# Gathered rows' vector operations pinned in source order, and the forget gates' sums moved behind the first heads' projections

## The chip, the cores and the metric

One core of one Trainium2 chip runs the whole program. The metric is the device time of one execution in microseconds (us). The engines are TensorE (PE, with its weight loads as PEld), VectorE (DVE), ScalarE (ACT), GpSimd (POOL) and SyncE (SP). Each runs its own instructions in a fixed order and waits at an instruction until what that needs is there.

## What is computed

Two transformer blocks over 512 tokens of width 1024 (D) behind 16 meta tokens. The part that matters first is the PEER layer: every token chooses 128 of 16384 experts (8 heads, 16 each); an expert is a row of the table u and a row of the table v. The first block ends with it; the second begins with a SwiGLU (ffn1) and then attention, eight heads of it with a forget gate.

```python
def peer_experts(xc, idx, gates, u, v):
    u_sel = jnp.take(u, idx, axis=0)
    act = jax.nn.gelu(jnp.einsum("chkd,cd->chk", u_sel, xc))
    v_sel = jnp.take(v, idx, axis=0)
    return jnp.einsum("chk,chkd->cd", act * gates, v_sel)
...
def fox_mixer(fq, fk, fv, f_logit, q_gain, k_gain, b_f):
...
    log_f = jax.nn.log_sigmoid((f_logit + b_f).astype(jnp.float32))
    c = jnp.cumsum(log_f, axis=1).transpose(0, 2, 1)
    out = blocked_causal_attention(to_heads(q), to_heads(k), to_heads(v), c)
    return from_heads(out)
...
        x = x + FFN_RESIDUAL_WEIGHT * swiglu(rms_norm_2(x, ffn1_norm[l]),
                                             ffn1_w_gate[l], ffn1_w_up[l], ffn1_w_down[l])
```

## The kernel before

**Three ways for four tiles.** The 512 tokens are four tiles of 128. Two of them pass through *all* experts on PE: 128 u tiles (L419, 128 experts each; the weights come as f32, ACT copies the high part into wh at L98, DVE subtracts it into wl at L103, and three products are summed) and 128 v tiles (`v_products`, the same three products), with the gates spread into a dense matrix between. The third tile (GT) has its chosen rows gathered: POOL issues an indirect DMA per choice (`fetch`, L564, 128 rows of u, then 128 of v, into four buffers named row), DVE multiplies a row of u with the token (`dot`, L570) or adds a weighted row of v to the token's sum (`add`, L580). After 16 dots ACT applies the gelu (L573). The fourth tile ("late") takes its activations out of the dense ones, which every fourth u tile spills to memory (act_d), by indirect DMAs into lact (L734); it gathers 128 rows of v (vrow, L755), and DVE adds them in `Late.add` (L744, L743 once in 16 rows). That goes on beside ffn1 and the first products of attention, until `last_tile` needs the sum.

**Stages.** Routing up to about 407 us. Then the gates stage, to about 600 us: 32 steps of eight tokens, each an oa (L622), eight ob (L625) and 16 small matmuls (L629) whose results ACT copies to stg, with u tiles between them. Then the loop: one u tile i+LAG and one v tile i per iteration, with LAG 36 (92 iterations, L668 makes the hidden values hf), and a load of gates, gt, of 1 MB every eighth iteration. SP issues the loads of weights and of gt in one queue. When the u tiles have run out, 36 iterations have v tiles alone (about 1327 to 1457 us). Behind it come the hand-over to ffn1 (a norm, whose dg at L817 PE needs), ffn1 on three tiles, the first products of attention, the late tile (about 1905 to 2045 us), and attention.

**What sets the order.** A scheduler puts each engine's instructions in order by a simulation of times, so an operation whose operand it believes to be there can go ahead of what the source has before it. `keep_in_program_order` keeps an instruction behind the one traced before it on its engine. Before, it is used for the gathers on POOL and the u tiles inside the gates stage, not for the operations that use the gathered rows. In the source the calls of `dot` and `add` are paced: one gather per step in the gates stage, then by `spent(n)`: at the loop's start 224 gathers are left, a u/v iteration counts 7 of 752 units and a v iteration 3. A row is used two gathers after its own.

**The forget gates.** In `attention`, the closures in `todo` finish the products of the last tile: `last(*todo[0])` the latents, `todo[1]` and `todo[2]` queries and keys of the gated heads, whose evacuation (`heads_norm`, L1169 to L1175: square fsq, sums, scale, four transposes) needs the scale r3m of the last tile; `todo[3]` their values. Between, DVE works off the latents' norm, the keys' rotation (krr) and a polynomial for the log of the gate (lf, up to L1251). `cp` (L1266) is the cumulative sum as four products with a triangle matrix, `c8` its copy, stored in cd (decay), and turned (L1271) into cq; both are read by the second eight heads.

Of the kernel before, what the change touches and what calls it, by code (L numbers as in the profile page):

```python
# [10 lines left out]
F32 = mybir.dt.float32  # L11
# [4 lines left out]
AF = mybir.ActivationFunctionType  # L16
ALU = mybir.AluOpType
# [3 lines left out]
P = 128  # L21
T = 512
# [410 lines left out]
def peer(c, A):  # L433
# [9 lines left out]
    with ExitStack() as es:  # L443
# [123 lines left out]

        def dot(row, s):
            jk = pe.tile([P, D], BF16, tag="jk", name="jkd", bufs=1)
            nc.vector.scalar_tensor_tensor(out=jk, in0=row, scalar=1.0, in1=xg, op0=ALU.mult, op1=ALU.mult, accum_out=gact[:, s:s + 1])  # L570
            if s % TOPK == TOPK - 1:
                hs = slice(s - TOPK + 1, s + 1)
                nc.scalar.activation(out=gact[:, hs], in_=gact[:, hs], func=AF.Gelu_apprx_tanh)  # L573

        def add(row, s):
            if s % TOPK == 0:
                hs = slice(s, s + TOPK)
                nc.vector.tensor_tensor(out=gwt[:, hs], in0=gact[:, hs], in1=G8[:, GT, s // TOPK, :], op=ALU.mult)
            hh = c.ht[GT]
            nc.vector.scalar_tensor_tensor(out=hh, in0=row, scalar=gwt[:, s:s + 1], in1=hh, op0=ALU.mult, op1=ALU.add)  # L580


        rows = []
# [135 lines left out]
class Late:  # L719
# [18 lines left out]
    def add(self):  # L738
        c, s = self.c, self.added
        if s % AHEAD == 0:  # L740
            hs = slice(s, s + AHEAD)
            a = c.lact[s // AHEAD]
            c.nc.vector.tensor_tensor(out=a, in0=a, in1=c.lg[:, hs], op=ALU.mult)  # L743
        c.nc.vector.scalar_tensor_tensor(out=self.h, in0=self.pending.pop(0), scalar=c.lact[s // AHEAD][:, s % AHEAD:s % AHEAD + 1], in1=self.h, op0=ALU.mult, op1=ALU.add)  # L744
        self.added += 1

    def steps(self, n):
# [321 lines left out]
def attention(c, A, late, late_cm):  # L1069
# [3 lines left out]
    def col(name, i=0, p=P):  # L1073
        o, n = CONST_COLS[name]
        return C[:p, o + i:o + i + 1]
# [3 lines left out]
    with ExitStack() as es:  # L1079
# [16 lines left out]
        def trp():  # L1096
            return pool.tile([P, 4, P], F32, tag="tr", name="tr", bufs=2)
# [19 lines left out]
        with tc.tile_pool(name="pre", bufs=1) as lq, tc.tile_pool(name="pret", bufs=2) as tp:  # L1117
# [30 lines left out]
            def last(w, n, evac, name="tm"):  # L1148

                ps = big(name)[:, 0:n]  # L1150
                for u in range(4):
                    wt = load_f(c, w[u], 2 * n)
                    for kk in range(2):
                        k = 2 * u + kk
                        nc.tensor.matmul(ps, xn[:, k, :], wt[:, kk * n:(kk + 1) * n], start=k == 0, stop=k == KD - 1)  # L1155
                evac(3, ps)
# [63 lines left out]
            rsqrt(c, l12, l12, (QR, KVR, ROPE))  # L1220
            for i, (o, n) in enumerate(parts):
                nc.vector.tensor_tensor(out=lat[:, :, o:o + n], in0=lat[:, :, o:o + n], in1=ls[:, i].unsqueeze(2).to_broadcast([P, 4, n]), op=ALU.mult)

            kr2 = tg.tile([P, T], F32, tag="z", name="kr2", bufs=1)
            kr = kr2[:, 0:4 * ROPE].rearrange("p (t d) -> p t d", t=4)
# [23 lines left out]
            nc.vector.tensor_tensor(out=y, in0=y, in1=z, op=ALU.mult)  # L1249
            nc.vector.tensor_scalar(out=lf, in0=lf, scalar1=0.0, scalar2=None, op0=ALU.min)  # L1250
            nc.vector.scalar_tensor_tensor(out=lf, in0=y, scalar=-2.0, in1=lf, op0=ALU.mult, op1=ALU.add)  # L1251
            last(*todo[1])
            for tt in range(4):
                ts = slice(tt * P, (tt + 1) * P)
                t4 = trp()
                nc.tensor.transpose(t4[:, 0, :], lat[:, tt, 0:P], c.ident)
                nc.tensor.transpose(t4[:QR - P, 1, :], lat[:, tt, P:QR], c.ident)
                nc.tensor.transpose(t4[:, 2, :], lat[:, tt, QR:QR + KVR], c.ident)
                for i, (p, oh, ol, g) in enumerate(((P, qnh[:, 0, ts], qnl[:, 0, ts], col("ql_g", 0)),
                                                    (QR - P, qnh[:QR - P, 1, ts], qnl[:QR - P, 1, ts], col("ql_g", 1, QR - P)),  # L1260
                                                    (P, kvh[:, ts], kvl[:, ts], col("kvl_g")))):
                    nc.scalar.activation(out=oh, in_=t4[:p, i, :], func=AF.Copy, scale=g)
                    nc.vector.scalar_tensor_tensor(out=ol, in0=t4[:p, i, :], scalar=g, in1=oh.bitcast(F32), op0=ALU.mult, op1=ALU.subtract)
            cp = big("cp")
            for j in range(4):
                nc.tensor.matmul(cp[:MH, j * P:], lf[:, j, :], tri[:, 0:T - j * P], start=(j == 0), stop=(j == 3), skip_group_check=True)  # L1266
            nc.scalar.mul(out=c8, in_=cp[:MH, :], mul=8.0)
            nc.sync.dma_start(out=cd, in_=c8)
            t4 = trp()
            for tt in range(4):  # L1270
                nc.tensor.transpose(t4[:, tt, 0:MH], c8[:, tt * P:(tt + 1) * P], c.ident[:MH, :MH])  # L1271
            nc.scalar.copy(out=cq, in_=t4[:, :, 0:MH])

            last(*todo[2])
            last(*todo[3])
            for ch in range(4):
                def evac(tt, ps):
                    z = tp.tile([P, T], F32, tag="t", name="z3", bufs=3)
# [19 lines left out]
                    nc.scalar.activation(out=dst[:, h0:h0 + 4, ts], in_=t4[:QF], func=AF.Copy, scale=col(g, 0, QF))  # L1298


            lat_cm.__exit__(None, None, None)
            wq0 = load_w(c, A["w_qb0"], n=768)
            wq1 = load_w(c, A["w_qb1"], n=768, p=QR - P)
            for tt in range(4):
# [29 lines left out]
            for tt in range(4):  # L1334
                ts = slice(tt * P, (tt + 1) * P)
                kt = tp.tile([P, MH, QF], F32, tag="qt", name="kt", bufs=2)
                ss = tp.tile([P, 2 * MH], F32, tag="ss8", name="kss", bufs=4)[:, 0:MH]
                pvs = []
                for half in range(2):
                    ps = pool.tile([P, 512], F32, tag=f"tm{tt % 2}", name="kp", bufs=1) if half else big("kp")  # L1340
                    s = slice(half * 512, half * 512 + 512)
                    mm3(nc, ps, kvh[:, ts], kvl[:, ts], wk[0][:, s], wk[1][:, s], True, True)
                    pv = ps.rearrange("p (h d) -> p h d", h=4)
                    sq = tp.tile([P, T], F32, tag="t", name="ksq", bufs=3)
                    sv = sq[:, 0:256].rearrange("p (h d) -> p h d", h=4)
                    nc.scalar.activation(out=sv, in_=pv[:, :, 0:NOPE], func=AF.Square)
                    nc.vector.tensor_reduce(out=ss[:, half * 4:half * 4 + 4], in_=sv, axis=AX.X, op=ALU.add)
                    pvs.append(pv)
                rsqrt(c, ss, ss, NOPE)
                for half, pv in enumerate(pvs):  # L1350
                    hs = slice(half * 4, half * 4 + 4)
                    nc.vector.tensor_tensor(out=kt[:, hs, 0:NOPE], in0=pv[:, :, 0:NOPE], in1=ss[:, hs].unsqueeze(2).to_broadcast([P, 4, NOPE]), op=ALU.mult)
                    nc.scalar.copy(out=vm[:, tt, hs, :], in_=pv[:, :, NOPE:])
                nc.gpsimd.tensor_copy(out=kt[:, :, NOPE:], in_=krr[:, tt:tt + 1, :].to_broadcast([P, MH, ROPE]))
                feature_major(kt, kT, "mk_g", ts)

        tp = es.enter_context(tc.tile_pool(name="att", bufs=2))
        msk = tp.tile([P, T], F32, name="msk", bufs=1)
# [240 lines left out]
```

## Time and profile before

| | |
|---|---|
| Median of 3 runs | 2746.47 us (2740.72 to 2750.86) |
| Profiled execution | 2757.47 us, its span 2755.7 us |
| Busy share of the span | PE 93%, PEld 76%, DVE 66%, ACT 33%, POOL 30% |
| Memory read and written | 534.05 MB and 31.47 MB |

A busy share is a mean over stages with different limits, so the views below cut the span into stretches. A row in the waits names the engine and line that waited, what it waited for, the sum, the number of times and the longest. In a timeline a bracket gives the idle time just ahead of an instruction and the instruction or DMA that ended it.

### The profile page before, as it was taken

How to read it: one execution, taken by the hardware profiler on the slowest of the kernel's cores; microseconds unless marked ns; L12 is line 12 of the kernel's file. 1: busy time of each engine (PE TensorE's matmuls, PEld its weight loads, DVE VectorE, ACT ScalarE, POOL GpSimd, SP SyncE). 2: the span in 40 equal slices, each digit the busy share in tenths (PEclk: the TensorE clock that was granted, in tenths of full speed). 3: DMA queues.
4: the chain of work that ended last, by engine and by line, in shares of the span. 5: the costliest groups of instructions: out<-in, count | busy, mean ns of one | idle time of the engine just before them, and what ended most of it. 6: DMA issues, size and time to landing. Idle time of an engine off the chain costs nothing. (4 is left out here: it accounts for less than half of the span.)

```text
span 2755.7 us, 33980 instructions
## 1 busy us (share of the span) xinstructions
PE 2556.0 (93%) x12098; PEld 2091.1 (76%) x12098; DVE 1812.1 (66%) x3710; ACT 915.6 (33%) x1531; POOL 823.9 (30%) x686
## 2 busy tenths in 40 slices
PE   8979988998999999999887998889988999999999
PEld 7955455787888888899666998877444877788887
DVE  7986996997878877644687987776013676443322
ACT  4232011543333333434344332333022554332221
POOL 0000244353444444100554787471000230211100
PEclk9989999999999999999998999999998799999999
DMA  4213137889999999755885888686875313222232
GB/s 169 95 61 101 62 107 276 298 284 332 345 333 339 333 324 334 268 170 178 257 282 198 292 270 279 219 293 222 299 256 169 102 36 108 90 94 94 96 103 75
DMA packets 196921, 567.77 MB, mean 206 GB/s; under 512 B 23240, under 2 KB 60488, under 8 KB 194576
## 3 DMA queue, kind: packets, MB, share of 16 engines
q1 hardware_dynamic: 132464, 355.60, 38.7%
q0 software_dynamic: 59392, 201.42, 21.1%
q10 hardware_dynamic: 4896, 8.57, 0.8%
q8 instruction: 96, 1.57, 0.2%
q14 instruction: 73, 0.60, 0.1%
HBM read 534.05 MB, written 31.47 MB: 205 GB/s over the span
## 5 line engine op out<-in xcount | busy, mean ns | idle before, releaser
L103 DVE TENSOR_TENSOR wl<-wf,wh 128x1024 fp32r<-128x1024 f32 (+2 forms) x438 | 533.7, 1219 | 276.5 <-ACT wh L98 270.5
L98 ACT CAST wh<-wf 128x1024 fp32r<-128x1024 f32 (+2 forms) x438 | 453.0, 1038 | 660.1 <-PE mm L80 207.5
L419 PE MATMUL u<-xh,wh 128*128 128x384 f32 x760 | 266.9, 351 | 33.0 <-ACT wh L98 33.0
L419 PE MATMUL u<-xh,wl 128*128 128x384 f32 x760 | 265.2, 349 | 8.5 <-DVE wl L103 8.5
L81 PE MATMUL mm<-hh,wl 128*128 128x384 f32 (+1 forms) x704 | 259.8, 369 | 8.1 <-DVE wl L103 8.0
L79 PE MATMUL mm<-hh,wh 128*128 128x384 f32 (+1 forms) x704 | 259.5, 370 | 7.2 <-ACT hh L793 3.5
L419 PE MATMUL u<-xl,wh 128*128 128x384 f32 x760 | 263.6, 347 | 0.0
L80 PE MATMUL mm<-hl,wh 128*128 128x384 f32 (+1 forms) x704 | 261.0, 371 | 0.0
L564 POOL DMA_INDIRECT row<-peer_u,gidx x128 | 180.3, 1408 | 242.4 <-DVE jkd L570 218.2
L734 POOL DMA_INDIRECT lact<-act_d,laid x128 | 157.4, 1230 | 243.9 <-DMA wf<-peer_v 205.3
L80 PE MATMUL v<-wl,hh 128*128 128x512 f32 x512 | 207.8, 406 | 15.7 <-DVE wl L103 15.3
L564 POOL DMA_INDIRECT row<-peer_v,gidx x128 | 165.1, 1290 | 179.1 <-DVE h_tok L580 151.5
L81 PE MATMUL v<-wh,hl 128*128 128x512 f32 x512 | 204.1, 400 | 0.0
L744 DVE SCALAR_TENSOR_TENSOR h_late<-vrow,lact,h_late 128x1024 f32<-128x1024 f32 x128 | 164.1, 1282 | 31.6 <-DMA vrow<-peer_v,lidx 30.9
L570 DVE SCALAR_TENSOR_TENSOR jkd<-row,xg 128x1024 bf16<-128x1024 f32 x128 | 158.2, 1236 | 38.8 <-DMA row<-peer_u,gidx 37.7
L419 PEld LDWEIGHTS u<-xh,wh 128*128 128x128 f32 x760 | 149.1, 196 | 40.5 <-ACT wh L98 36.5
L419 PE MATMUL u<-xf,w 128*128 128x384 f32 x496 | 172.7, 498 | 7.3 <-ACT spill L427 7.3
L580 DVE SCALAR_TENSOR_TENSOR h_tok<-row,gwt,h_tok 128x1024 f32<-128x1024 f32 x128 | 164.1, 1282 | 21.7 <-DMA row<-peer_v,gidx 21.2
L755 POOL DMA_INDIRECT vrow<-peer_v,lidx x128 | 153.1, 1196 | 54.9 <-issue 25.3
L419 PEld LDWEIGHTS u<-xh,wl 128*128 128x128 f32 x760 | 148.8, 196 | 14.3 <-DVE wl L103 14.0
L79 PE MATMUL v<-wh,hh 128*128 128x512 f32 x512 | 157.0, 400 | 2.5 <-ACT wh L98 2.5
L525 POOL TENSOR_TENSOR dk<-CE,posf 128x800 f32<-128x800 f32 x32 | 48.7, 1552 | 353.6 <-DVE posf L521 353.6
(437 smaller groups left out, 5311.8 us busy)
## 6 DMA issues: line engine op xcount, KB each, us to landing
wf<-peer_v SPq DMA_DIRECT2D x128, 512.0 KB, 4.6
wf<-u_t SPq DMA_DIRECT2D x95, 512.0 KB, 5.4
wf<-f_g SPq DMA_DIRECT2D x44, 512.0 KB, 3.4
wf<-f_u SPq DMA_DIRECT2D x44, 512.0 KB, 3.5
w<-u_t SPq DMA_DIRECT2D x33, 512.0 KB, 4.0
gates_d<-stg SPq DMA_DIRECT2D x16, 1024.0 KB, 7.0
gt<-gates_d SPq DMA_DIRECT2D x16, 1024.0 KB, 12.4
wf<-f_d SPq DMA_DIRECT2D x32, 512.0 KB, 3.7
```

What stands on the lines that cost most here:

```text
L79: nc.tensor.matmul(ps, lh, rh, start=start, stop=False)
L80: nc.tensor.matmul(ps, lh, rl, start=False, stop=False)
L81: nc.tensor.matmul(ps, ll, rh, start=False, stop=stop)
L98: nc.scalar.copy(out=h, in_=f)
L103: (nc.vector if lo == "v" else nc.gpsimd).tensor_tensor(out=l, in0=f, in1=h.bitcast(F32), op=ALU.subtract)
L419: mm = nc.tensor.matmul(ps3, l, r, start=k == 0 and m == 0, stop=k == KD - 1 and m == len(mms) - 1)
L564: dm = nc.gpsimd.indirect_dma_start(out=row, out_offset=None, in_=src, in_offset=bass.IndirectOffsetOnAxis(ap=gidx[:, s:s + 1], axis=0))
L570: nc.vector.scalar_tensor_tensor(out=jk, in0=row, scalar=1.0, in1=xg, op0=ALU.mult, op1=ALU.mult, accum_out=gact[:, s:s + 1])
L580: nc.vector.scalar_tensor_tensor(out=hh, in0=row, scalar=gwt[:, s:s + 1], in1=hh, op0=ALU.mult, op1=ALU.add)
L734: dm = c.nc.gpsimd.indirect_dma_start(out=c.lact[s // AHEAD][:, s % AHEAD:s % AHEAD + 1], out_offset=None, in_=acts, in_offset=bass.Indire ...
L744: c.nc.vector.scalar_tensor_tensor(out=self.h, in0=self.pending.pop(0), scalar=c.lact[s // AHEAD][:, s % AHEAD:s % AHEAD + 1], in1=self.h, ...
L755: dm = c.nc.gpsimd.indirect_dma_start(out=row, out_offset=None, in_=self.A["peer_v"], in_offset=bass.IndirectOffsetOnAxis(ap=c.lidx[:, s:s ...
```

## The change

The operations of `dot`, `add` and `Late.add` get `keep_in_program_order`, and in `attention` the calls `last(*todo[1])`, `last(*todo[2])`, the transposes of the latents and `last(*todo[3])` move ahead of the keys' rotation and the polynomial, and the cumulative sum moves behind the projections of the keys (`kp`). No instruction is added or removed. In lines of after, L570 stays, L580 is L581, L622 is L624, L668 is L670, L744 is L746, L1155 to L1203 are three higher.

```diff
         def dot(row, s):
             jk = pe.tile([P, D], BF16, tag="jk", name="jkd", bufs=1)
-            nc.vector.scalar_tensor_tensor(out=jk, in0=row, scalar=1.0, in1=xg, op0=ALU.mult, op1=ALU.mult, accum_out=gact[:, s:s + 1])
+            op = nc.vector.scalar_tensor_tensor(out=jk, in0=row, scalar=1.0, in1=xg, op0=ALU.mult, op1=ALU.mult, accum_out=gact[:, s:s + 1])
+            tc.keep_in_program_order(op)
...
             hh = c.ht[GT]
-            nc.vector.scalar_tensor_tensor(out=hh, in0=row, scalar=gwt[:, s:s + 1], in1=hh, op0=ALU.mult, op1=ALU.add)
+            op = nc.vector.scalar_tensor_tensor(out=hh, in0=row, scalar=gwt[:, s:s + 1], in1=hh, op0=ALU.mult, op1=ALU.add)
+            tc.keep_in_program_order(op)
...
-        c.nc.vector.scalar_tensor_tensor(out=self.h, in0=self.pending.pop(0), scalar=c.lact[s // AHEAD][:, s % AHEAD:s % AHEAD + 1], in1=self.h, op0=ALU.mult, op1=ALU.add)
+        op = c.nc.vector.scalar_tensor_tensor(out=self.h, in0=self.pending.pop(0), scalar=c.lact[s // AHEAD][:, s % AHEAD:s % AHEAD + 1], in1=self.h, op0=ALU.mult, op1=ALU.add)
+        c.tc.keep_in_program_order(op)
         self.added += 1
...
                 nc.vector.tensor_tensor(out=lat[:, :, o:o + n], in0=lat[:, :, o:o + n], in1=ls[:, i].unsqueeze(2).to_broadcast([P, 4, n]), op=ALU.mult)
+            last(*todo[1])
+            last(*todo[2])
+            for tt in range(4):
+                ts = slice(tt * P, (tt + 1) * P)
+                t4 = trp()
+                nc.tensor.transpose(t4[:, 0, :], lat[:, tt, 0:P], c.ident)
...
+            last(*todo[3])
 
             kr2 = tg.tile([P, T], F32, tag="z", name="kr2", bufs=1)
...
             nc.vector.scalar_tensor_tensor(out=lf, in0=y, scalar=-2.0, in1=lf, op0=ALU.mult, op1=ALU.add)
-            last(*todo[1])
-            for tt in range(4):
...
-            cp = big("cp")
...
-            last(*todo[2])
-            last(*todo[3])
...
                 feature_major(kt, kT, "mk_g", ts)
+            cp = big("cp")
+            for j in range(4):
+                nc.tensor.matmul(cp[:MH, j * P:], lf[:, j, :], tri[:, 0:T - j * P], start=(j == 0), stop=(j == 3), skip_group_check=True)
+            nc.scalar.mul(out=c8, in_=cp[:MH, :], mul=8.0)
+            nc.sync.dma_start(out=cd, in_=c8)
...
+            lat_cm.__exit__(None, None, None)
```

DVE at the start of the gates stage, before (jkd is the discarded product of a dot, gact its sum; a count at the end is of the same instruction in a row):

```order
L554 SCALAR_TENSOR_TENSOR laid<-ef,ea 128x128
L570 SCALAR_TENSOR_TENSOR jkd,gact<-row,xg 128x1024 x3
L622 TENSOR_TENSOR oa<-iota,sT 128x1024
L625 TENSOR_SCALAR ob<-iota,sT 128x128 x8
L622 TENSOR_TENSOR oa<-iota,sT 128x1024
L625 TENSOR_SCALAR ob<-iota,sT 128x128 x8
L570 SCALAR_TENSOR_TENSOR jkd,gact<-row,xg 128x1024 x10
L622 TENSOR_TENSOR oa<-iota,sT 128x1024
L625 TENSOR_SCALAR ob<-iota,sT 128x128 x8
L570 SCALAR_TENSOR_TENSOR jkd,gact<-row,xg 128x1024 x3
L578 TENSOR_TENSOR gwt<-gact,G_2044 128x16
L570 SCALAR_TENSOR_TENSOR jkd,gact<-row,xg 128x1024 x7
```

The same place after:

```order
L554 SCALAR_TENSOR_TENSOR laid<-ef,ea 128x128
L624 TENSOR_TENSOR oa<-iota,sT 128x1024
L627 TENSOR_SCALAR ob<-iota,sT 128x128 x8
L624 TENSOR_TENSOR oa<-iota,sT 128x1024
L627 TENSOR_SCALAR ob<-iota,sT 128x128 x8
L570 SCALAR_TENSOR_TENSOR jkd,gact<-row,xg 128x1024
L624 TENSOR_TENSOR oa<-iota,sT 128x1024
L627 TENSOR_SCALAR ob<-iota,sT 128x128 x8
L570 SCALAR_TENSOR_TENSOR jkd,gact<-row,xg 128x1024
```

Up to the fourth oa 23 dots stood before, and two stand now; from there each oa is followed by one. Over the stage 59 dots stood ahead of the first hf before, 35 now.

DVE in the loop at its 80th v tile, before (hf and hl are the hidden values' parts, wl a weight's low part; numbers tell the tiles apart):

```order
L668 TENSOR_TENSOR hf_9962<-act_7608,gt_9505 128x256
L103 TENSOR_TENSOR wl_9737<-wf_9734,wh_9736 128x1024
L103 TENSOR_TENSOR wl_9777<-wf_9774,wh_9776 128x1024
L103 TENSOR_TENSOR hl_9900<-hf_9897,hh_9899 128x256
L668 TENSOR_TENSOR hf_10029<-act_7675,gt_10027 128x256
L103 TENSOR_TENSOR wl_9803<-wf_9800,wh_9802 128x1024
```

The same place after:

```order
L670 TENSOR_TENSOR hf_9962<-act_7608,gt_9505 128x256
L581 SCALAR_TENSOR_TENSOR h_tok_92<-row_9724,gwt_2047,h_tok_92 128x1024
L103 TENSOR_TENSOR wl_9777<-wf_9774,wh_9776 128x1024
L581 SCALAR_TENSOR_TENSOR h_tok_92<-row_9727,gwt_2047,h_tok_92 128x1024
L103 TENSOR_TENSOR hl_9900<-hf_9897,hh_9899 128x256
L103 TENSOR_TENSOR wl_9803<-wf_9800,wh_9802 128x1024
L581 SCALAR_TENSOR_TENSOR h_tok_92<-row_9730,gwt_2047,h_tok_92 128x1024
L670 TENSOR_TENSOR hf_10029<-act_7675,gt_10027 128x256
```

Before, dots and adds came at some 2.7 per hf up to the 73rd, where 101 adds were done, and then none up to the 97th. After, they come at 2.1 per hf from the first hf to the 97th.

PE behind the late tile, before (tm products of `last`, ss the last tile's sum of squares, tl the latents, cp the cumulative sum):

```order
L1203 MATMUL ss<-ones,sqs 128x1
L1175 MATMUL tr<-ident,fsq 128x128 x4
L1256 MATMUL tr<-ident,tl 128x128
L1257 MATMUL tr<-ident,tl 64x128
L1258 MATMUL tr<-ident,tl 128x128
```

The same place after:

```order
L1206 MATMUL ss<-ones,sqs 128x1
L1158 MATMUL tm<-w_16240,xn 128x512 x2
L1158 MATMUL tm<-w_16244,xn 128x512 x2
L1158 MATMUL tm<-w_16248,xn 128x512 x2
L1158 MATMUL tm<-w_16252,xn 128x512 x2
L1178 MATMUL tr<-ident,fsq 128x128 x4
L1158 MATMUL tm<-w_16319,xn 128x512 x2
```

Sixteen products that do not need the sum of squares now stand between it and the latents' transposes, eight of them ahead of the first fsq transposes. The four cp products, which stood eight rows behind the sum of squares, come some 200 rows later.

## Rows read from the trace of the kernel before

**Rows 1.** Page, busy time by engine: us, share of the span, instructions.
```profile
PE 2556.0 (93%) x12098; PEld 2091.1 (76%) x12098; DVE 1812.1 (66%) x3710; ACT 915.6 (33%) x1531; POOL 823.9 (30%) x686
```

**Rows 2.** Stretches: length, busy PE, PEld, DVE, ACT, POOL (instructions), PEclk, DMA share, GB/s.
```profile
485.00:600.00 115.00, 115.00 (x634) 87.46 (x633) 115.00 (x291) 58.78 (x83) 51.46 (x27) 1.00 0.85 295
630.00:1146.00 516.00, 478.99 (x2345) 435.04 (x2344) 410.45 (x513) 191.72 (x335) 211.20 (x167) 0.96 0.93 331
1146.00:1327.00 181.00, 181.00 (x932) 166.72 (x931) 85.08 (x103) 73.34 (x130) 0.00 (x0) 1.00 0.58 181
1327.00:1480.00 153.00, 131.06 (x540) 102.92 (x539) 117.26 (x169) 65.27 (x102) 80.93 (x65) 0.93 0.74 241
```

**Rows 3.** Line L419 in 630 to 1146, then 1146 to 1327: min/median/max ns.
```profile
L419 PE MATMUL u<-xh,wh x518: 331/340/689, 629.5 to 1145.8; 128*128 128x384 f32 x173
...
L419 PE MATMUL u<-xh,wh x206: 334/340/343, 1145.8 to 1323.4; 128*128 128x384 f32 x103
```

**Rows 4.** Waits in 630 to 1146: us in total, times, longest.
```profile
POOL row L564 <- DVE h_tok L580: 151.0, 80, 9.9
...
PE u L419 <- ACT wh L98: 33.0, 8, 6.0
...
ACT wh L98 <- DMA wf<-u_t: 29.3, 17, 4.7
```

**Rows 5.** DMA, 600 to 1150 (last row: 1146 to 1327): queue shares; issues, us to landing.
```profile
q0 software_dynamic: 25488, 92.81, 46.6%
...
q1 hardware_dynamic: 40400, 83.14, 43.6%
...
gt<-gates_d SPq DMA_DIRECT2D x10, 1024.0 KB, 13.3
...
row<-peer_v,gidx POOLq DMA_INDIRECT x101, 7.7
...
gt<-gates_d SPq DMA_DIRECT2D x4, 1024.0 KB, 7.3
```

**Rows 6.** PE's timeline, 455 to 486: start, us, [idle <-releaser]; a wait of ACT.
```profile
456.67 7.12 PE L419 MATMUL u<-xf,w 128*128 128x384 f32 x16 [4.31 <-ACT spill L427]
...
464.07 2.75 PE L419 MATMUL u<-xf,w 128*128 128x384 f32 x8
...
477.01 3.78 PE L629 MATMUL g<-ob,oa 128*128 128x128 f32 x16 [6.05 <-DVE ob L625]
...
483.40 1.95 PE L629 MATMUL g<-ob,oa 128*128 128x128 f32 x16
...
ACT gact L573 <- DVE jkd L570: 18.3, 3, 14.7
```

**Rows 7.** Waits in 1327 to 1480; then a DVE group: busy, mean ns, idle.
```profile
DVE h_tok L580 <- DMA row<-peer_v,gidx: 17.1, 8, 7.1
...
PE v L80 <- DVE wl L103: 15.3, 9, 4.2
...
L580 DVE SCALAR_TENSOR_TENSOR h_tok<-row,gwt,h_tok 128x1024 f32<-128x1024 f32 x27 | 34.7, 1286 | 17.2 <-DMA row<-peer_v,gidx 17.1
```

**Rows 8.** Timelines of PE and DVE at the hand-over to ffn1.
```profile
1499.54 1.62 PE L818 MATMUL bc<-dg,ones 128*128 128x128 f32 x6 [11.27 <-DVE dg L817]
...
1492.18 1.28 DVE L744 SCALAR_TENSOR_TENSOR h_late<-vrow,lact,h_late 128x1024 f32<-128x1024 f32 x1 [5.66 <-DMA vrow<-peer_v,lidx]
```

**Rows 9.** Waits of PE in ffn1, 1510 to 1790.
```profile
PE dn L81 <- DVE wl L103: 13.8, 6, 4.8
PE mm L81 <- DVE wl L103: 8.0, 2, 5.8
```

**Rows 10.** PE's timeline before attention's last tile.
```profile
1862.19 1.12 PE L1175 MATMUL tr<-ident,fsq 128*128 128x128 f32 x4 [8.10 <-DVE fsq L1172]
```

**Rows 11.** PE's timeline behind the late tile.
```profile
2067.51 1.09 PE L1175 MATMUL tr<-ident,fsq 128*128 128x128 f32 x4 [11.77 <-DVE krr L1066]
...
2071.32 3.95 PE L1266 MATMUL cp<-tl,lf 128*8 128x512 f32 x6 [1.04 <-DVE lf L1251]
```

More of the change, by code (lines that the diff above doesn't have):

```diff
@@ L1222, in attention @@
                 nc.vector.tensor_tensor(out=lat[:, :, o:o + n], in0=lat[:, :, o:o + n], in1=ls[:, i].unsqueeze(2).to_broadcast([P, 4, n]), op=ALU.mult)
+            last(*todo[1])
[4 more added lines that the diff above has]
+                nc.tensor.transpose(t4[:, 0, :], lat[:, tt, 0:P], c.ident)
+                nc.tensor.transpose(t4[:QR - P, 1, :], lat[:, tt, P:QR], c.ident)
+                nc.tensor.transpose(t4[:, 2, :], lat[:, tt, QR:QR + KVR], c.ident)
+                for i, (p, oh, ol, g) in enumerate(((P, qnh[:, 0, ts], qnl[:, 0, ts], col("ql_g", 0)),
+                                                    (QR - P, qnh[:QR - P, 1, ts], qnl[:QR - P, 1, ts], col("ql_g", 1, QR - P)),
+                                                    (P, kvh[:, ts], kvl[:, ts], col("kvl_g")))):
+                    nc.scalar.activation(out=oh, in_=t4[:p, i, :], func=AF.Copy, scale=g)
+                    nc.vector.scalar_tensor_tensor(out=ol, in0=t4[:p, i, :], scalar=g, in1=oh.bitcast(F32), op0=ALU.mult, op1=ALU.subtract)
+            last(*todo[3])
             kr2 = tg.tile([P, T], F32, tag="z", name="kr2", bufs=1)
@@ L1251, in attention @@
             nc.vector.scalar_tensor_tensor(out=lf, in0=y, scalar=-2.0, in1=lf, op0=ALU.mult, op1=ALU.add)
-            last(*todo[1])
-            for tt in range(4):
[L1254 to L1263, printed above, removed]
-            cp = big("cp")
[L1265 to L1272, printed above, removed]
-            last(*todo[2])
-            last(*todo[3])
             for ch in range(4):
@@ L1298, in feature_major @@
                     nc.scalar.activation(out=dst[:, h0:h0 + 4, ts], in_=t4[:QF], func=AF.Copy, scale=col(g, 0, QF))
-            lat_cm.__exit__(None, None, None)
             wq0 = load_w(c, A["w_qb0"], n=768)
@@ L1355, in attention @@
                 feature_major(kt, kT, "mk_g", ts)
+            cp = big("cp")
[3 more added lines that the diff above has]
+            nc.sync.dma_start(out=cd, in_=c8)
+            t4 = trp()
+            for tt in range(4):
+                nc.tensor.transpose(t4[:, tt, 0:MH], c8[:, tt * P:(tt + 1) * P], c.ident[:MH, :MH])
+            nc.scalar.copy(out=cq, in_=t4[:, :, 0:MH])
+            lat_cm.__exit__(None, None, None)
         tp = es.enter_context(tc.tile_pool(name="att", bufs=2))
```

## Prediction

> **What bounds the kernel now.** I read the page first: TensorE (PE) is busy 93% of the span [rows 1], so only two things can bring time: its idle stretches, and its work at the lower clock. The table of stretches says where these are [rows 2]. From 485 to 600 us PE and VectorE (DVE) are both busy without a gap; from 630 to 1146 PE is busy 478.99 of 516 us at a granted clock of 0.96; from 1146 to 1327 it is busy throughout at 1.00. The two last stretches run the same loop (one u tile and one v tile per iteration). Of the matmul u<-xh,wh, eight belong to one u tile: 518 in the first stretch are 64.75 iterations of **7.97 us**, 206 in the second are 25.75 of **7.03 us** [rows 3]. The only difference is that in the first POOL gathers rows (211 us busy) and in the second it does nothing [rows 2]. So gathering costs 64.75 × 0.94 = 61 us, though no row is an operand of a matmul.
>
> How it costs is in the waits: PE waits 33.0 us in 8 long waits for wh of a u tile, and ScalarE's copy into wh waits 29.3 us for the weights' DMA wf<-u_t [rows 4]. Eight long waits in 64 iterations is the beat of the gt load (1 MB every eight iterations, in the same queue as the weights). It lands in 13.3 us where rows are gathered and in 7.3 where none are [rows 5]. The DMA engines are busy 93% of the first stretch, 58% of the second [rows 2]; queue q0 (the gathers) holds 46.6% of their time and q1 (weights, gt) 43.6% [rows 5]. The rows are fetched too fast early, and then the engines have room that nothing uses. The pace comes from DVE: POOL waited 151.0 us for L580 to free a row buffer [rows 4], so whoever spaces DVE's dots and adds spaces the gathers.
>
> **1. Gates stage: −12 us (0 to −15).** Before, ten dots stand between two of the first oa operations, then ten more; DVE sits on late rows there, gelu L573 waits 14.7 us for a dot, and behind it the spill copy that frees PE's bank: PE waits 4.31 us for L427 and 6.05 us for ob L625 [rows 6]. After, one dot follows each oa. DVE had exactly that mix from 485 to 600, where both engines are full [rows 2], and PE's own order is unchanged in this stage, so the waits go: 10.4 us. The 16 u matmuls behind the first wait took 7.12 us, more than twice the 2.75 of eight; the 16 gate products behind the second took 3.78 against 1.95 later [rows 6]: 3.4 us more. I take 12 of 13.8. It is 0 if the ob operations turn out to set the pace there anyway.
>
> **2. The u/v loop: −45 us (−61 to +24).** Source order paces rows: 224 remain at the loop's start, 7 of 752 units fall to a u/v iteration, so 2.085 rows per iteration instead of 2.58 (POOL's 167 gathers in 64.75 iterations [rows 2]), now through all iterations. Time of the 16 engines per iteration before: 0.93 × 7.97 = 7.41 us [rows 2], of it 0.466 × 7.97 = 3.71 for the rows in q0 [rows 5]. After, q0 falls to 3.71 × 2.085/2.58 = 3.00, the sum to 6.70 us. That is below PE's 7.03, so PE can set the pace (90.5 × 7.03 = 636 us against 697 from 630 to 1327: −61). But before, the engines were used to 93%; at the same use 6.70 needs **7.2 us**, which I take: 652 us, −45. DVE fits: 410.45 us in 64.75 iterations is 6.34 each [rows 2]; less 0.5 rows at 1.29 [rows 7] that is 5.7. The other end is in rival A.
>
> **3. The v-only tail (1327 to about 1457): −8 us (−17 to +8).** POOL sent its last 27 u/v rows in a burst there; DVE waited 17.1 us for them and PE 15.3 us for wl behind those waits [rows 7]. Spread rows need not be waited for. Against that, counted in the new order, 33 adds instead of 27 stand in the tail: 6 × 1.29 = 7.7 us on an engine busy 117 of 153 us [rows 2]. 17 − 8 is 9; I take 8. If no wait goes and the adds come on top it is +8.
>
> **4. Hand-over to ffn1: −4 us (0 to −9).** PE waits 11.27 us for dg L817 [rows 8], and three Late adds stand in DVE's chain to it (3 × 1.28 = 3.8 [rows 8]). They move behind it. The first, which waits for its row, stays in front.
>
> **5. ffn1: −10 us (+5 to −20).** Here PE waits 13.8 + 8.0 = 21.8 us for wl [rows 9], always with a Late add or L743 waiting ahead of it on DVE for a gather. Most adds now stand about three weights later, so the row waits should shrink, but L743 keeps its place, and with it the waits for the last of 16 activations. So half. A row that is later still puts wl behind it: +5, one wait of the longest kind.
>
> **6. Before attention's last tile: −6 us (+5 to −11).** PE waits 8.10 us for the fsq chain of the first head products [rows 10] with nine Late adds among its small steps; after, no add stands there. But the last 14 adds move behind, and the late tile's transposes depend on the last one, with no gate products left to cover it. I take 8 less a 2 us wait.
>
> **7. Forget gates: −10 us (−5 to −12).** After the late tile PE waits 11.77 us, because the fsq transposes stand in its order behind a long DVE chain (r3m, latents, k-rope, polynomial), then 1.04 for lf, and the cumulative sum runs slowly behind it: 3.95 us for six small products [rows 11]. After, 16 products of last(todo[2]) and last(todo[3]) stand before and between the transposes, and the sum moves behind the kv heads, whose other waits cover its DVE steps. The products are ready as r3m is needed only by their evacuation. No DMA is added; the decay store comes 34 rows later in SP's queue, still ahead of its first reader (cbs, for the second eight heads), and behind it wait only loads for later stages.
>
> **The sum.** 12 + 45 + 8 + 4 + 10 + 6 + 10 = 95 us. The profiled execution took 2757.5 us (span 2755.7), 0.4% above the median 2746.5; 95 off the median is **2651 us**.
>
> **Rival A: the loop stays short of DMA.** The row: q0 and q1 hold nearly equal shares (46.6% and 43.6%) [rows 5]. If weights get no more than that share while a row is on its way, and now in every iteration one is (2.085 rows × 7.7 us landing is 16 us of flight per iteration), then each iteration takes 7.97 us to the end: 90.5 × 7.97 = 721 us, +24 instead of −45. Milder: only the eight long waits stay, 33.0/8 = 4.1 us per eight iterations, 7.03 + 0.52 = 7.55, 683 us, −14. With the tail at 0 and ffn1 at −5 the other terms give 37, so the whole is −51 to −13: I put it at −32, **2714 us**. For it: the landing times. Against it: q0's demand is set by DVE's pace, and what it leaves goes to the weights, whereas before a gather always stood ready.
>
> The Trainium skill, "DMA: Bandwidth & Descriptors", section "Queues, rings and completion order", says that each DMA engine takes packets in turn from the queues that have work. By that rule alone weights get half an engine's time whenever a gather is queued, which is rival A; the trace's shares of 46.6% and 43.6% agree with it, but no row here shows what a gather that comes at a slower pace leaves.
>
> **Rival B, slower: DVE blocks behind a late row.** Four row buffers make a circle: gather issued (1.26 us of POOL, 211.20/167 [rows 2]), landing 7.7, add 1.29: 10.25 us for four rows, 2.6 per row, where the loop asks one per 7.2/2.085 = 3.45. With the position fixed, DVE can no longer do other work first, so a circle above 4 × 3.45 = 13.8 us (a landing above 11.3) slows the loop and every wl with it. It decides for slower when it eats the other terms too (50 us): 747 us, 8.25 per iteration, a circle of 15.8, a landing of 13.3 us. At 14 us: 16.55/4 × 2.085 = 8.63 × 90.5 = 781 us, +84 − 50 = +34: **2780 us**. Against: 7.7 was the median at 93% use, and the gathers become fewer per time.
>
> **Rival C: no change.** The same bytes and the same DVE work remain, so PE's gaps may close in one place and open in the next: every term at its bad end, with the milder loop of A, gives 0 − 14 + 8 + 0 + 5 + 5 − 5 = −1: **2745 us**. That the pins do nothing is excluded by the order, which moves 24 dots out of the gates stage.
>
> **How the numbers follow.** Forecast 0.64 (terms near their values, −60 to −140), rival A 0.23, C 0.08, B 0.05. The range takes the forecast's good side (loop at 7.03 and half of the other waits more: about −138) to past the middle of A: 2608 to 2722. About 0.5% (14 us) is what a measurement can tell from none. Faster: 0.64 and 0.21 of A, 0.85; same: C and the rest of A, 0.10; slower: B, 0.05.
>
> **What would show it.** In the profile of after: u/v iterations of 7.0 to 7.3 us to the end, POOL busy until about 1270, DMA share even at 0.92 to 0.96, gt landing below 12 us; no wait of PE above 3 us at the gates; the L570 and L580 waits for rows reduced to a few us; about 3 us or less where 11.77 stood, and the cumulative sum behind the kv heads. I am wrong if iterations stay near 8 us (A), if L580 waits for rows in every iteration (B), or if the tail grows by what the loop gains (C).

## The result, and the profile after

The changed kernel takes 2638.5 us (median, 2634.1 to 2645.4) against 2748.7 for the kernel before beside it: a ratio of **0.960** (0.956 to 0.964), 110 us less. The forecast was 2651 in a range of 2608 to 2722. A second set of runs gave 0.959 (0.957 to 0.961).

Three lines of the page of after: busy time of the engines (as [rows 1] before), then the granted clock of PE and the DMA's busy share, each in 40 slices of the span in tenths.

```profile
PE 2520.9 (96%) x12098; PEld 2066.8 (78%) x12098; DVE 1803.5 (68%) x3710; ACT 919.4 (35%) x1531; POOL 793.7 (30%) x686
...
PEclk9989999999999999999999999999998999999999
...
DMA  4222224889999999999986888687874214222232
```

PE is busy 96% of a span of 2636.6 us instead of 93%. The clock's digits stand below 9 in two slices, where before it was four, and the DMA row keeps its nines to the end of the u/v loop and one slice into the v-only tail.

Stretches of after (columns as in [rows 2]): the first steps of the gates stage, the u/v loop, the tail.

```profile
408.00:485.00 77.00, 77.00 (x328) 51.52 (x327) 39.78 (x100) 22.90 (x42) 12.63 (x9) 1.00 0.61 205
...
610.00:1253.00 643.00, 637.64 (x3254) 585.20 (x3253) 505.74 (x653) 263.66 (x457) 224.99 (x190) 0.99 0.93 332
...
1253.00:1380.00 127.00, 113.84 (x459) 87.79 (x459) 106.80 (x141) 54.94 (x80) 84.70 (x62) 0.95 0.88 300
```

PE has no gap left at the start of the gates stage. In the loop PE is busy 637.64 of 643 us at a clock of 0.99, where it was 478.99 of 516 at 0.96 [rows 2], and the DMA share is the same 0.93 as before. POOL now spreads its gathers over the whole loop (190 in this stretch).

To see where the 110 us came from I take the time between landmarks of PE (first or last instruction of a kind, from the line views), in the two traces of before and after and in a second pair from another set of runs:

| stage | before | after | difference | second pair | forecast |
|---|---|---|---|---|---|
| gates stage (routing's end to first u<-xh) | 188.3 | 173.3 | −15.0 | −15.8 | −12 |
| u/v loop (to last u) | 727.2 | 671.2 | −56.0 | −41.2 | −45 |
| v-only tail (to last v) | 132.8 | 124.4 | −8.4 | −9.8 | −8 |
| hand-over and ffn1 (to first tm) | 336.9 | 310.0 | −26.9 | −19.2 | −14 |
| to the late tile's sum of squares | 262.0 | 263.3 | +1.3 | −1.6 | −6 |
| to the last product lg of the gated heads | 226.1 | 213.5 | −12.6 | −14.5 | −10 |
| whole span | 2755.7 | 2636.6 | −119.1 | −102.6 | −95 |

### The profile page after: what moved, and what is told of

It is laid out like the page before. It is cut to its first block, busy times and chain, and to the rows that moved or that the text cites. A ratio compares the mean times of both kernels' runs of the same rounds, so it can differ in the third digit from the quotient of the medians.

```text
span 2636.6 us, 33993 instructions
## 1 busy us (share of the span) xinstructions
PE 2520.9 (96%) x12098; PEld 2066.8 (78%) x12098; DVE 1803.5 (68%) x3710; ACT 919.4 (35%) x1531; POOL 793.7 (30%) x686
## 4 chain that ended last, share of the span: by engine, by line
PE 75%; DVE 10%; DMA 7%; issue 4%; POOL 2%; ACT 2%; SPq 0%; ACTq 0%; DVEq 0%; POOLq 0%
PE u L419 18%; PE mm L80 4%; PE mm L79 4%; PE mm L81 4%; PE v L80 3%; PE v L79 3%; PE v L81 3%; PE x L989 3%; DMA wf<-u_t 3%; DMA vrow<-peer_v,lidx 2%; PE dn L81 2%; PE dn L79 2%; PE dn L80 2%; PE g L631 2%; PE pj L79 2%
## 5 line engine op out<-in xcount | busy, mean ns | idle before, releaser
L564 POOL DMA_INDIRECT row<-peer_u,gidx x128 | 162.1, 1266 | 344.6 <-DVE jkd L570 332.6
L419 PE MATMUL u<-xh,wh 128*128 128x384 f32 x760 | 259.5, 341 | 2.7 <-ACT wh L98 2.6
L419 PE MATMUL u<-xh,wl 128*128 128x384 f32 x760 | 257.4, 339 | 2.7 <-DVE wl L103 2.7
L419 PE MATMUL u<-xl,wh 128*128 128x384 f32 x760 | 257.2, 338 | 0.0
L79 PE MATMUL v<-wh,hh 128*128 128x512 f32 x512 | 167.6, 402 | 5.7 <-ACT wh L98 5.7
L419 PE MATMUL u<-xf,w 128*128 128x384 f32 x496 | 171.1, 494 | 1.9 <-ACT spill L427 1.9
L746 DVE SCALAR_TENSOR_TENSOR h_late<-vrow,lact,h_late 128x1024 f32<-128x1024 f32 x128 | 163.8, 1280 | 9.6 <-DMA vrow<-peer_v,lidx 8.9
L581 DVE SCALAR_TENSOR_TENSOR h_tok<-row,gwt,h_tok 128x1024 f32<-128x1024 f32 x128 | 163.6, 1278 | 7.8 <-DMA row<-peer_v,gidx 7.7
L736 POOL DMA_INDIRECT lact<-act_d,laid x128 | 150.4, 1175 | 48.7 <-issue 35.8
L570 DVE SCALAR_TENSOR_TENSOR jkd<-row,xg 128x1024 bf16<-128x1024 f32 x128 | 156.8, 1225 | 0.8 <-DMA row<-peer_u,gidx 0.7
L419 PEld LDWEIGHTS u<-xh,wh 128*128 128x128 f32 x760 | 143.7, 189 | 8.6 <-ACT wh L98 4.0
L79 PEld LDWEIGHTS mm<-hh,wh 128*128 128x128 f32 x704 | 132.6, 189 | 20.8 <-ACT hh L796 2.4
```

Of the source, the lines that this page charges most:

```text
L79: nc.tensor.matmul(ps, lh, rh, start=start, stop=False)
L419: mm = nc.tensor.matmul(ps3, l, r, start=k == 0 and m == 0, stop=k == KD - 1 and m == len(mms) - 1)
L564: dm = nc.gpsimd.indirect_dma_start(out=row, out_offset=None, in_=src, in_offset=bass.IndirectOffsetOnAxis(ap=gidx[:, s:s + 1], axis=0))
L570: op = nc.vector.scalar_tensor_tensor(out=jk, in0=row, scalar=1.0, in1=xg, op0=ALU.mult, op1=ALU.mult, accum_out=gact[:, s:s + 1])
L581: op = nc.vector.scalar_tensor_tensor(out=hh, in0=row, scalar=gwt[:, s:s + 1], in1=hh, op0=ALU.mult, op1=ALU.add)
L736: dm = c.nc.gpsimd.indirect_dma_start(out=c.lact[s // AHEAD][:, s % AHEAD:s % AHEAD + 1], out_offset=None, in_=acts, in_offset=bass.Indire ...
```

## Experiments

My theory: the change works through the *pace* at which DVE frees row buffers, so that gathers no longer take DMA time that weights need; the Late pin and the attention move are small and separate. The rivals: a gather that is still queued keeps the weights short (A), DVE blocks behind late rows (B), and, for the mechanism, that the burst of the gt load alone made the waits, or that the fixed order as such did.

**One part at a time.** The pins on `dot` and `add` alone (the first two edits of the change):

> Only dot and add of the third tile are pinned; Late.add and attention are as before. My theory (the pins set the pace of the gathers, and the pace is worth the gates stage, the u/v loop and the tail): these three stages take what they took in the changed kernel, 188, 671 and 124 us between the same PE landmarks against 188 + 15, 727 and 133 before, so -79 us, about 2669 us; ffn1 and attention as before. Rival (the gain in the loop needs the Late pin too, because all of them are one order on DVE): less than half of it, about 2710 us.

Measured: 0.972 (0.968 to 0.976), −78 us beside its before of 2769; the gates stage took 173.3, the loop 672.2 us, both as in the changed kernel, the tail 129.7. The rival is out: the loop's gain needs nothing else. Then the pin in `Late.add` alone:

```diff
-        c.nc.vector.scalar_tensor_tensor(out=self.h, ...
+        op = c.nc.vector.scalar_tensor_tensor(out=self.h, ...
+        c.tc.keep_in_program_order(op)
```

> Only Late.add is pinned. If hand-over and ffn1 are its own work: -27 us there and +1 before the late tile, nothing in the u/v loop, about 2721 us. Rival (the hand-over and ffn1 went faster because the tail before them left the late rows earlier, that is because of the peer pins): under 10 us, above 2738 us.

Measured: 0.993 (0.990 to 0.996), −20 us; the loop unchanged at 725.7. Hand-over and ffn1 took 330.8 us. On the same chip, with Late as before, they took 346.5 in the run with the attention move alone and 340 in that with the peer pins alone: −9 to −16, and +6 against the first of them from there to the sum of squares. With all pins they took 310 and 320 in the changed kernel, but 331 and 336 in two runs below whose ffn1 code is the same and where only the loop and the tail differ. So the Late pin alone gives a part of the 27, and what the stages ahead of ffn1 leave behind matters too: the rival isn't out. Then the move in attention alone:

> Only the move in attention. Theory: the wait of 11.77 us on the fsq transposes goes and the cumulative sum costs 2 us instead of 4: -12 us between the late tile's sum of squares and the heads, about 2736 us, and nothing elsewhere. Rival (the waits move on to the projections of the query): within 5 us of before.

Measured: 0.995 (0.992 to 0.997), −14 us; from the sum of squares to the heads 210.3 us against 226.1. The three ratios multiply to 0.9718 × 0.9929 × 0.9948 = 0.960, the ratio of the whole change: in sum the parts add up, within intervals of 0.2 to 0.4% each.

**The pace.** All pins stay, and only the spacing changes:

```diff
-            GSPAN = 4 * EARLY + 7 * (NE - LAG) + 3 * (LAG - 4)
+            GSPAN = 580
```

> The changed kernel with all three pins, but the 224 rows of the loop spaced over 580 units instead of 752: 2.7 rows per u/v iteration, all used by the 83rd, as before the change, and none in the tail. If the pace is what counts: the 16 DMA engines are asked for 7.4 us per iteration again, iterations of 7.5 to 8 us up to the 83rd, loop +40 to +60 us, tail -10 to -20, about 2670 us. Rival (the fixed place itself helps, since DVE does no work out of turn): the loop stays at 7.03 us per iteration, and with the shorter tail about 2625 us.

Measured: 0.986 (0.982 to 0.989): some 70 us of the 110 are gone. The loop took 733.2 us, +62. How the iterations stand is read from L670, one hf each (first and last start), and from the waits in the loop:

```profile
L670 DVE TENSOR_TENSOR hf<-act,gt x62: 412/424/427, 714.4 to 1194.0; 128x256 f32<-128x256 f32 x62
...
PE u L419 <- ACT wh L98: 40.1, 10, 6.7
...
DVE jkd L570 <- DMA row<-peer_u,gidx: 5.5, 6, 2.0
...
DVE h_tok L581 <- DMA row<-peer_v,gidx: 0.7, 1, 0.7
```

From the first to the last of 62 hf, 479.6 us, it is 7.86 us per iteration, as before the change, with the waits for wh back (40.1 us in ten), while DVE waits only 6 us for rows in the whole loop. POOL issued 162 gathers in these 61 iterations, 2.66 each; before, it was 133 in the 50 iterations from 703 to 1099 us, 2.66 as well. The same pace gives the same time, pinned or not. So the pins without the pace give nothing in the loop, and rival B is not what limits it. The tail took 125 us without an add; 11.8 us of that are one wait for wh whose cause the trace doesn't name.

> The changed kernel with a v-only iteration counted as 1 unit instead of 3: 2.28 rows per u/v iteration, 0.33 in the tail. Demand 3.70 + 3.71 x 2.28/2.58 = 6.98 us of DMA per iteration. Theory (the engines give about 94% of their time, as in the runs with 2.6 and 2.7 rows): 7.42 us per iteration, the loop +20 to +36 us against the changed kernel, the tail, which took 125 us without any add as well, unchanged: ratio 0.967 to 0.973. Rival (only a demand above PE's time counts): loop unchanged, ratio 0.96, or below it if the tail gains.

```diff
-            GSPAN = 4 * EARLY + 7 * (NE - LAG) + 3 * (LAG - 4)
+            GSPAN = 4 * EARLY + 7 * (NE - LAG) + 1 * (LAG - 4)
...
-                spent(4 * EARLY + 3 * (i + 1) + 4 * min(i + 1, NE - LAG))
+                spent(4 * EARLY + 7 * min(i + 1, NE - LAG) + max(i + 1 - (NE - LAG), 0))
```

Measured: 0.964 (0.960 to 0.967). The same views as above:

```profile
L670 DVE TENSOR_TENSOR hf<-act,gt x68: 408/425/428, 703.4 to 1198.7; 128x256 f32<-128x256 f32 x68
...
PE u L419 <- ACT wh L98: 13.0, 4, 5.9
```

495.3/67 = 7.39 us per iteration, against 7.42 expected, and four of the long waits are back; the loop took 694.7 us, 15 more than in the changed kernel beside it. But the tail fell to 109.0 from 121.3, with 14 adds in it instead of 31, which I had not expected; so the ratio came out below the 0.967 to 0.973 of the theory. Three runs with this weight have a tail of 109 to 111 us. That it is the adds that cost is not shown: the run just above had none there and took 125. Loss and gain nearly cancel.

**Burst or mean demand.** In the kernel before, the gt load in eight pieces:

```diff
-                    nc.sync.dma_start(out=gt, in_=gd[:, :, i:i + GRP, :].rearrange("g p e t -> p g (e t)"))
...
+                e0, q0 = (i // GRP + 1) * GRP, 2 * (i % GRP)
+                if e0 < NE:
+                    nc.sync.dma_start(out=ahead[:, q0:q0 + 2, :], in_=gd[q0:q0 + 2, :, e0:e0 + GRP, :].rearrange("g p e t -> p g (e t)"))
```

> The kernel before, with the gt load of 1 MB every eighth iteration split into eight loads of 128 KB, one per iteration, a group ahead; all bytes and all other operations as before. Theory (the mean demand of 7.41 us of DMA per iteration is over PE's 7.03, and the long waits at the gt load only show the backlog): the eight long waits dissolve into short ones, the loop gains under 20 us, ratio 0.99 to 1.00. Rival (the burst itself makes the waits): the loop falls from 727 towards 675 us, ratio about 0.98.

Measured: 0.991 (0.988 to 0.994), loop 710.6 against 720.6 in the before beside it. L675 holds the hf there:

```profile
L675 DVE TENSOR_TENSOR hf<-act,gt x52: 411/424/445, 703.3 to 1092.0; 128x256 f32<-128x256 f32 x52
...
PE v L79 <- ACT wh L98: 8.8, 6, 2.1
...
PE u L419 <- ACT wh L98: 5.4, 5, 1.2
```

The long waits dissolved, as the theory has it: 388.7/51 = 7.62 us per iteration instead of 7.91 (7.94 in the before beside it). The burst is worth 0.3 us. The other 0.6 above PE's 7.03 stays without it, at the same 2.7 rows per iteration and with the DMA engines busier than in any other loop (last two columns: 0.96, 346 GB/s):

```profile
703.00:1092.00 389.00, 370.75 (x1832) 332.55 (x1831) 320.93 (x389) 148.29 (x258) 175.27 (x136) 0.98 0.96 346
```

That this rest is the mean demand is inferred from the pace: it is 0.36 us at 2.28 rows above, and 0.05 at 2.09 in the changed kernel below.

> The run with 1 unit per v-only iteration, with the gates' loads in eighths added. That run lost about 15 to 23 us in the loop and won 12 to 15 in the tail. If the loss came from the burst of the gt load on a queue without slack (four waits for wh, 13.0 us), the loop falls back to 675 to 682 us and the tail stays at 109: ratio 0.956 to 0.958. If the mean demand sets it, the loop stays at 690 or above: ratio 0.962 to 0.964.

Measured: 0.964 (0.963 to 0.966); loop 686.4, tail 111.3. The loop fell between the two cases, so this run doesn't tell burst from demand; the total is that of the run without eighths.

**ffn1 and the late tile.**

```diff
-            if self.acts < min(NE, self.rows + AHEAD):
+            if self.acts < min(NE, self.rows + 2 * AHEAD):
```

> The changed kernel with the late tile's activations fetched 32 rows ahead instead of 16. In the changed kernel L745 still waits four times, 20.6 us in all, for the last of its 16 activations, and three of PE's waits for wl (7.9 us) lie behind it. Theory (L745 holds DVE and so PE's weights): its waits fall under 5 us and ffn1 gains 5 to 8 us, ratio 0.957. Rival (PE's waits come from the late rows, L746, or the DMA as such): within 3 us of the changed kernel, ratio 0.959 to 0.960.

Measured: 0.961 (0.959 to 0.962), no gain. Waits of PE and DVE in hand-over and ffn1, then of PE up to the late tile:

```profile
PE mm L81 <- DVE wl L103: 2.0, 1, 2.0
...
PE dn L81 <- DVE wl L103: 1.3, 1, 1.3
...
DVE lact L745 <- DMA lact<-act_d,laid: 21.2, 3, 8.1
...
PE tr L942 <- issue: 10.4, 1, 10.4
...
PE tr L1178 <- DVE fsq L1175: 8.2, 1, 8.2
```

PE's waits for wl fell to 3.3 us, but not because L745 waits less (21.2 us still), and 8.2 us on the fsq chain came back with 10.4 at the late tile: that stretch took 142.1 us against 128.2. So the theory isn't confirmed: L745's waits did not fall under 5 us, and the time came back further on.

```diff
-STEP = 3520
+STEP = 3200
```

> The changed kernel with the late tile's steps every 3200 columns of PE instead of 3520, so that four adds instead of 14 stand behind the last fsq chain. Theory (my step that failed: PE waits 9.9 us at the late tile's transposes for the last adds, which nothing covers): that wait falls to 3 us or less, ratio 0.957. Rival (denser gathers cost ffn1 as much, since the DMA is at 0.84 there): ratio 0.960 or above.

Measured: 0.969 (0.967 to 0.971), slower than the changed kernel. DVE just ahead of the late tile, then the last third of ffn1 in this run and in the changed kernel of another set (stretches, columns as in [rows 2]):

```profile
1855.26 0.56 DVE L1112 TENSOR_TENSOR zt<-gate,rs 128x384 f32<-128x384 f32 x1 [5.03 <-DMA gate_z<-zt]
...
1855.73 5.24 DVE L746 SCALAR_TENSOR_TENSOR h_late<-vrow,lact,h_late 128x1024 f32<-128x1024 f32 x4
...
1597.00:1728.00 131.00, 104.41 (x531) 99.03 (x530) 89.12 (x94) 31.03 (x42) 94.74 (x83) 0.87 0.78 259
...
1598.00:1702.00 104.00, 95.77 (x530) 94.27 (x529) 78.69 (x85) 32.13 (x43) 73.60 (x65) 0.97 0.82 281
```

Four adds instead of 14 stand behind the chain, and the wait at L942 fell only from 9.9 to 7.2 us; what holds it is shown below. The same 530 products took 131 us instead of 104, at a clock of 0.87, with 83 gathers beside them instead of 65. The gathers came no faster, 0.63 per us in both, so it looks as if the stage now lasts as long as its gathers do; that is argued from this one stretch and not tested further.

> All of the above in one kernel: eighths, 1 unit per v-only iteration, activations 32 ahead, steps of 3200 columns. If each works on its own stage, the ratios multiply: 0.957 x 0.957 x 0.957 / 0.9597^2, about 0.952. If they compete for the DMA in tail and ffn1, no better than the best of the three.

Measured: 0.969 (0.967 to 0.971). Its loop took 690 us, its tail 110, hand-over and ffn1 347; the runs above have 686 and 111 (eighths with 1 unit) and 346 (steps of 3200). So each part did here what it did there, and the loss is that of the shorter steps; that the parts compete is not shown. No version beat the changed kernel. The second pair in the table comes from a repeat of before (2752.9 us, one execution) and of after (0.959 of its before):

> The kernel before once more, for a trace from the same chip as the runs beside it: the stages differ by a few us from the first trace, most in ffn1, where the same code took 337 us in the first trace and 346 in the run with the attention move alone.

> The changed kernel once more beside the others: 0.956 to 0.964 of before. If the pins in the PEER layer, the Late pin and the attention move add up as their single ratios do (0.9718 x 0.9929 x 0.9948 = 0.9599), the ratio is 0.96 again.

## Why the prediction was right, and where it was not

**Gates stage, right.** −15 for −12; PE has no idle gap there, where before 66.47 of the 77 us from 408 to 485 were busy, at a clock of 0.93. All runs with the peer pins took 173.3 to 173.5 us.

**The loop: right in cause, mis-sized.** Iterations after and before, from the hf operations:

```profile
L670 DVE TENSOR_TENSOR hf<-act,gt x70: 409/418/427, 708.3 to 1196.7; 128x256 f32<-128x256 f32 x70
...
L668 DVE TENSOR_TENSOR hf<-act,gt x51: 410/424/428, 703.3 to 1098.9; 128x256 f32<-128x256 f32 x51
```

488.4/69 = 7.08 us against 395.6/50 = 7.91. I had 7.2, since I reckoned the demand at 6.70 us and held the DMA engines to 93% of use. The share in the loop is 0.93 again, but at 7.08: the demand is 6.6. My rows per iteration were a mean over a stretch too long, 2.58; from 703 to 1099 they were 2.66, and the queue of the gathers held more (columns as in [rows 5]):

```profile
q0 software_dynamic: 19162, 69.78, 48.5%
```

0.485 × 7.91 = 3.84 us for 2.66 rows make 3.01 for 2.085; with the other 3.60 of 7.44 (a share of 0.94 there) the sum would have been 6.6. The floor of 7.03 is nearly reached. The second trace has −41, so 45 lies inside what two traces differ by.

What a wait for weights costs is more than its length. Of the 0.94 us that an iteration with gathers took longer, 0.57 were idle time of PE, (516 − 478.99)/64.75; the other 0.37 were PE's own work, 7.40 us busy instead of 7.03 [rows 2]. PE ran slower behind each of the eight long waits: the first matmul there took 0.44 to 0.69 us. One of them, before (timeline; then a stretch, its clock in the third column from the end):

```profile
663.62 0.69 PE L419 MATMUL u<-xh,wh 128*128 128x384 f32 x1 [4.49 <-ACT wh L98]
...
662.00:668.70 6.70, 4.83 (x14) 4.33 (x15) 5.07 (x7) 2.10 (x2) 2.16 (x2) 0.50 0.59 213
```

Behind these 4.49 us without work the granted clock was 0.50, 1.2 GHz instead of 2.4, and a matmul that takes 0.34 us took 0.52 to 0.69. In the loop after, with 637.64 of 643 us busy, the clock is 0.99. The prediction had both parts in its 7.97 and 7.03, without telling them apart.

What changed is seen at ACT, which fills wh; waits in the loop after, and one of before:

```profile
ACT wh L98 <- DMA wf<-u_t: 62.8, 29, 7.0
...
ACT wh L98 <- PE u L419: 52.1, 19, 2.9
...
PE u L419 <- ACT wh L98: 2.6, 2, 1.3
```

```profile
ACT wh L98 <- PE u L419: 2.9, 1, 2.9
```

Before, ACT found a free wh buffer at once except once (2.9 us): no stock of weights was in hand. After, it waits 52.1 us for PE to free one: weights stand ready between gt loads. The gt load itself still lands late, and ACT even waits longer for weights (62.8 us in 643 against 29.3 in 516 [rows 4]); but that time comes out of the stock, and PE waits 2.6 us instead of 33.0. DMA queues and landings of after, as [rows 5]:

```profile
q1 hardware_dynamic: 52694, 109.29, 48.6%
...
q0 software_dynamic: 27487, 100.11, 42.2%
...
gt<-gates_d SPq DMA_DIRECT2D x12, 1024.0 KB, 12.8
...
row<-peer_v,gidx POOLq DMA_INDIRECT x100, 7.7
```

My marker "gt landing below 12 us" was wrong: 12.8 for 13.3. Rows land in the same 7.7 us. Rival A falls with the shares: q0 fell from 46.6% to 42.2%, q1 rose from 43.6% to 48.6%. What the gathers no longer ask for goes to the weights. The Trainium skill ("DMA: Bandwidth & Descriptors", "Queues, rings and completion order") says that an engine goes round the queues that have work, packet by packet. Half of an engine's time, as the prediction has it, was my own step from that rule; no equal shares came of it here.

**Tail, right in sum.** −8.4 and −9.8 for −8, by waits that shrank (17.1 and 15.3 us in [rows 7]); 31 adds stand there, where I had counted 33:

```profile
DVE h_tok L581 <- DMA row<-peer_v,gidx: 6.8, 6, 2.3
...
PE v L80 <- DVE wl L103: 6.6, 4, 2.4
...
PE v L79 <- ACT wh L98: 5.7, 2, 4.0
```

But runs with the tail's code as before took 126.6 to 132.8 us, and the run with the peer pins alone, with its new code, 129.7, so the sum is not clear of that spread.

**Hand-over right, ffn1 mis-sized.** Waits from the last v to the first tm:

```profile
PE dn L81 <- DVE wl L103: 7.9, 3, 4.2
...
PE bc L821 <- DVE dg L820: 7.6, 1, 7.6
...
DVE lact L745 <- DMA lact<-act_d,laid: 20.6, 4, 9.0
...
DVE h_late L746 <- DMA vrow<-peer_v,lidx: 8.9, 4, 5.6
```

dg: 11.27 to 7.6, the −4 of step 4. The waits for wl went from 21.8 to 7.9 us, −14 where I took half, −10 (23.8 to 12.8 in the second pair). L745 did keep its waits as I said (20.6 us, 24.0 before); those for the rows fell from 27.7 to 8.9. The whole stage, before and after (stretches, columns as in [rows 2]):

```profile
1457.00:1793.50 336.50, 296.08 (x1627) 291.21 (x1627) 262.88 (x323) 111.70 (x159) 225.87 (x179) 0.95 0.76 253
...
1377.60:1687.20 309.60, 289.62 (x1627) 286.61 (x1625) 258.71 (x319) 111.96 (x159) 210.63 (x179) 0.97 0.81 275
```

PE's idle time fell from 40.4 to 20.0 us, most of it the two waits; the other 6.5 of the 27 are the same 1627 products done in less time, at a clock of 0.97 for 0.95. Steps 4 and 5 counted waits alone and had no term for that. The second pair has −19 in all, so the size of this gain is the least certain of the larger ones.

**Before the late tile, wrong.** Step 6 said 8 us less a wait of 2 for the last adds; the stage gained nothing. The fsq wait did go, from 8.10 to 0.2 us, but the wait that I had put at 2 us is 9.9, at the late tile's transposes. DVE and PE there, after:

```profile
1795.13 2.60 DVE L746 SCALAR_TENSOR_TENSOR h_late<-vrow,lact,h_late 128x1024 f32<-128x1024 f32 x2
...
1809.58 0.56 DVE L1112 TENSOR_TENSOR zt<-gate,rs 128x384 f32<-128x384 f32 x1 [7.71 <-DMA gate_z<-zt]
...
1810.05 5.24 DVE L746 SCALAR_TENSOR_TENSOR h_late<-vrow,lact,h_late 128x1024 f32<-128x1024 f32 x4
...
1815.39 1.94 PE L942 MATMUL tr<-ident,h_late 128*128 128x128 f32 x8 [9.89 <-issue]
```

The last four adds had their rows. They stood behind zt L1112 of the last gate product, and that waited 7.71 us for the *store* of the zt before it, which has one buffer. The pin keeps the adds behind it. Before, the last add ran ahead of both, and PE came to the transposes (L939) without a gap:

```profile
1887.28 1.28 DVE L744 SCALAR_TENSOR_TENSOR h_late<-vrow,lact,h_late 128x1024 f32<-128x1024 f32 x1
...
1919.43 0.56 DVE L1109 TENSOR_TENSOR zt<-gate,rs 128x384 f32<-128x384 f32 x1 [5.02 <-PE gate L81]
...
1925.92 0.56 DVE L1109 TENSOR_TENSOR zt<-gate,rs 128x384 f32<-128x384 f32 x1 [5.93 <-DMA gate_z<-zt]
...
1909.99 0.82 PE L939 MATMUL tr<-ident,h_late 128*128 128x128 f32 x6
```

I had counted the adds behind the chain and not looked at what else is queued ahead of them on DVE. The run with the Late pin alone shows the same:

```profile
1912.66 0.56 DVE L1110 TENSOR_TENSOR zt<-gate,rs 128x384 f32<-128x384 f32 x1 [7.26 <-DMA gate_z<-zt]
...
1918.48 1.94 PE L940 MATMUL tr<-ident,h_late 128*128 128x128 f32 x8 [9.44 <-issue]
```

So do all nine traces with the Late pin: zt waits 5.0 to 8.2 us for the store, four adds follow, and PE waits 7.2 to 10.4 us. In the five without it zt waits as well (5.8 to 10.2 us), but the adds are done by then and PE has no gap there. A second buffer for zt was not tried.

**Forget gates, right.** −12.6 and −14.5 for −10, a little past the end of its range (−12). Waits of PE after, from the sum of squares to the heads:

```profile
PE qp L79 <- DVE qt L1317: 7.0, 1, 7.0
...
PE tm L1158 <- ACT tl L1163: 2.1, 1, 2.1
...
PE tr L1178 <- ACT fsq L1171: 0.7, 1, 0.7
```

The 11.77 and 1.04 [rows 11] are gone, and 7.0 at the query's projections (7.4 before) is what was there already.

So the 95 of the sum stand against 119 in one pair of traces, 103 in the other and 110 in the medians: the gates stage and attention gave 3 to 5 us more than their steps, ffn1 13 and 5, the loop 11 more and 4 less, and one small step gave nothing. That the total came so close to the forecast is in part luck: the surplus of ffn1 covers the step that failed.

## What to carry to other kernels

Where a background stream of gathers shares DMA with a loop's weights, add up the engine time that an iteration asks for and compare it with the compute engine's floor; spread the stream until the sum lies clearly below that, and let it last as long as the loop: 6.6 us against 7.03 was enough here, 0.93 × 7.39 = 6.9 was not. A scheduler that moves the consumers of gathered rows ahead changes the stream's pace, and with it when other transfers land. Pinning the order has its price: each pinned operation waits for whatever stands ahead of it, so look for a wait on a single-buffered store there.

## What the runs showed of the hardware

In the loops with gathers the DMA engines were 0.92 to 0.94 busy, at 328 to 337 GB/s, whether PE waited or not; in the kernel before with the gates' loads in eighths they reached 0.96 and 346 GB/s. So the share alone doesn't say whether they limit. Iterations took 7.08 us with 2.09 rows, 7.39 with 2.28, 7.86 and 7.91 with 2.66 (pinned and not), in line with the demand. PE had a granted clock of 0.99 in the first of these loops and 0.96 in the last two; after a wait of 4.5 us it was 0.50. And hand-over and ffn1 of one and the same code took 337, 340 and 346 us in three traces.
